# Linear attention: extra turns ahead of the first and last products, two block sums of the feed-forward weights made one column group earlier, and w_out split further ahead

## The chip, the cores and the metric

The kernel runs on one core of one Trainium2 chip. The metric is the time of one execution on the device in microseconds (us); lower is better. The times of a kernel are given as the median of its runs.

## The reference

One encoder layer on x of 512 x 2048 in float32. Cut to what matters:

```python
h = rmsnorm(x, attn_norm_w); proj = h @ w_in          # split: aq, ak, av, gq, gk, gv, gr, glr
attn_out = mixture_of_dilations(aq, ak, av)           # 16 heads of 64, three window patterns
log_a = log_sigmoid(glr @ gate_w + gate_b) / 16       # one for each direction, per key column
# gated linear attention, 4 heads, key width 128, value width 256, both directions summed:
#   S_t = diag(a_t) S_{t-1} + k_t^T v_t ;  o_t = q_t S_t
gla_out = rmsnorm_per_head(fwd + bwd) * gla_norm_w * silu(gr)
x = x + concat([attn_out, gla_out]) @ w_out           # w_out: 2048 x 2048
h = rmsnorm(x, ffn_norm_w)
x = x + (silu(h @ w_gate) * (h @ w_up)) @ w_down      # hidden width 5632
return rmsnorm(x, final_norm_w)
```

## The kernel before

**Products.** A float32 operand is split into two rounded halves, hi and lo, and a product is made as hi·hi + hi·lo + lo·hi: three matmuls, for the output jobs lines L346, L347 and L348. The hi half is a copy on ScalarE (ACT, L237), the lo half a subtraction on VectorE (DVE, L218). L347 is the matmul that reads the lo half of the weight. Gate and up, later, use products of blocks that are first added up; the sums of a weight piece are `Blocks.sums` (DVE, L1414 to L1416), its halves `Blocks.split` (ACT L1427, DVE L1432).

**Stages.** The attention's v projection to about 95 us; further projections of w_in to 345; attention and the linear attention's q, k and v projections to 612; the output projection to 843; gate and up to about 1715; down and the last norm to the end. The change lies in the output projection. It has column groups of 512 columns, each with 16 row blocks k. The first half of k (the attention's part) of groups 1, 2 and 3 comes first (612 to 715 us), then group 0 whole (to 770), then the second half of k (the linear attention's part) of groups 1, 2 and 3 (770 to 794, 794 to 817, 817 to 843). One step i of a job takes one k through four banks, so four units of three matmuls each. A job's banks are added to the residual by DVE (L1302, four of them, in `evac_out`).

**What runs beside it.** The four heads of linear attention are generators, `gla(h)`. `turns(…, APART)` interleaves them with a distance of 12 turns; after each bank of a job the rate (`RATES`) gives a quarter of so many turns, so a `yield` in `gla` is a place where other work is put in between, on every engine. A head does in this order: gate logits on TensorE (PE, L923); Abs, Exp, Ln on ACT (L933 to L935) with L936 on DVE; `less` (L945), `scan` (L951), `centre` (L963 to L966), exponents (ACT L973 to L975), `times` (L982) on DVE; for each direction the **first products** L1015 and transposes L1018 on PE, masked by L1021 on DVE and copied by ACT (L1025), added by L1029; `sums` (L1040 on PE), `decays` (L1049 on ACT), `chain` (L1059 on DVE); the **last products** L1087 on PE; squares and the norm (ACT L1095, DVE L377 to L386, ACT L1103); eight transposes L1110 on PE and the gate by L1113 on DVE; and the halves of the result (DVE L902), urgent. v comes back from DRAM by `load_gv` (POOL, L855).

Another side job makes block sums of later weights and stores them in DRAM (DVE L1483, POOL L1485).

**What sets the order.** Each engine runs its queue in the order in which the program issued it. Which bank of PSUM (`ps`) or buffer a step gets is decided when the program is built, by which one was put back first. `Job.lead(i)` says how many halves of the weight are split ahead of step i; `AHEAD` is 3. `before_out(c)` is called ahead of each step of the second halves and places gate's and up's loads (`ff.load`, SyncE L1395), sums and splits; a call of `ff.sums` on halves is six DVE instructions.

Of the kernel before, what the change touches and what calls it, by code (L numbers as in the profile page):

```python
# [26 lines left out]
KT = D // P  # L27
# [85 lines left out]
def put(*slots):  # L113
    for s in slots:
        if s.home is not None:
            s.home.free.append(s.i)


def layer(nc, tc, x, attn_norm_w, w_in, rel_table, gw_f, gb_f, gw_b, gb_b, gla_norm_w, w_out,
# [7 lines left out]
    with tc.manual_schedule(), \  # L127
# [43 lines left out]
        def tables(name):  # L171
            if state["set"] != name:
                state["set"] = name
                act.preload_act_table_set(name)
# [69 lines left out]
        AHEAD = 3  # L244

        def piece512(w, col, kt):

            ws = w if isinstance(w, list) else [(w, col)]
            n = 512 // len(ws)
            segs = []  # L250
            for i, (wi, c) in enumerate(ws):
                src = wi[kt * P:(kt + 2) * P, c:c + n].rearrange("(k p) c -> p k c", p=P)
                segs.append((src, lambda t, i=i, n=n: t.rearrange("p (k c) -> p k c", k=2)[:, :, i * n:(i + 1) * n]))
            return segs
# [9 lines left out]
        def run_urgent():  # L264
            while urgent:
                try:
                    next(urgent[0])
                    break
                except StopIteration:
                    urgent.popleft()  # L270
# [26 lines left out]
        def job(kind, pieces, kts, acts, evac, rate=0.0, before=None, start=None, limit=None):  # L297

            j = Job()
            j.kind, j.kts, j.acts, j.evac, j.rate, j.before, j.start, j.limit = \  # L300
                kind, kts, acts, evac, rate, before, start, limit
            j.first = len(st.halves)
            st.add(pieces)
            j.n = len(st.halves) - j.first
            jobs.append(j)
            return j
# [205 lines left out]
        def squares(c, t, tiles, ss, at_=None):  # L512
            junk = s2.get()
            m = c + (4 * t if at_ is None else at_)
            act.activation(junk.t, tiles[t].t, AF.Square, accum_out=ss[:, m:m + 1])
            put(junk)
# [314 lines left out]
        def evac_gqk(pr):  # L831
            def f(banks):
                for i in range(4):
                    t = s2.get()
                    if i < 2:
                        dve.scalar_tensor_tensor(t.t, banks[i].t, P ** -0.5, rb[1].t,
                                                 op0=OP.mult, op1=OP.mult)
                    else:
                        dve.tensor_tensor(t.t, banks[i].t, rb[1].t, op=OP.mult)
                    put(banks[i])  # L840
                    pool.dma_start(out=gqd[4 * pr + i], in_=t.t)
                    put(t)
            return f
# [69 lines left out]
        def gla(h):  # L913
# [15 lines left out]
            for d in range(2):  # L929
                tables(EXP_LN)  # L930
                bcol = wcol[:, (B_F, B_B)[d] + h:(B_F, B_B)[d] + h + 1]
                l, m = s2.get(), s2.get()
                act.activation(l.t, zs[d].t, AF.Abs, bias=bcol)  # L933
                act.activation(l.t, l.t, AF.Exp, scale=-1.0)
                act.activation(l.t, l.t, AF.Ln, bias=1.0)  # L935
                dve.tensor_scalar(m.t, zs[d].t, bcol, 0.0, op0=OP.add, op1=OP.min)  # L936
                put(zs[d])
                las.append((m, l))
                yield
            fs = [sc[d][:, 0:3] for d in range(2)]  # L940
            gs, qs, ks = [], [], []

# [68 lines left out]
            for d in range(2):  # L1011
                a, tr = ps.get(), ps.get()
                for b in range(4):
                    c = slice(b * P, (b + 1) * P)
                    mm(a.t[:, c], ks[d].t[:, c], qs[d].t[:, c], start=True, stop=True)  # L1015
                for b in range(4):
                    c = slice(b * P, (b + 1) * P)
# [37 lines left out]
            def chain(d):  # L1055
                for n, b in list(enumerate(orders[d]))[1:]:
                    at_ = b if d == 0 else b - 1
                    s = stts[d].t[:, n]
                    dve.scalar_tensor_tensor(s, stts[d].t[:, n - 1], fs[d][:, at_:at_ + 1], s,  # L1059
                                             op0=OP.mult, op1=OP.add)  # L1060
# [7 lines left out]
            decays(1)  # L1068
            yield
            chain(1)  # L1070
            yield

            on = s4.get(F32, [P, 4, 256])
# [3 lines left out]
            for i in range(2):  # L1077
                o = ps.get()
                for b in (2 * i, 2 * i + 1):
                    c = slice(b * P, (b + 1) * P)  # L1080
# [19 lines left out]
            for i in range(2):  # L1100
                for b in (2 * i, 2 * i + 1):
                    c = slice((b % 2) * 256, (b % 2 + 1) * 256)
# [120 lines left out]
                fr.late()  # L1223

        n_front = len(jobs)
        RATES = (2.5, 4.0)
        APART = 12
        for pr in range(2):
            seg = [(w_in, C_GQ + pr * 256), (w_in, C_GK + pr * 256)]
            job("A", [piece512(seg, None, k) for k in range(0, KT, 2)], list(range(KT)), acts_h,  # L1230
                evac_gqk(pr), rate=RATES[0], start=gstart if pr == 0 else None,
                before=None if pr else before_first, limit=3)
            job("B", [piece512(w_in, C_GV + pr * 512, k) for k in range(0, KT, 2)], list(range(KT)), acts_h,
                evac_gv(pr), rate=RATES[0],
                before=(lambda i: load_gates() if i == 12 else None) if pr else None)
# [63 lines left out]
        def evac_out(c, part=False):  # L1299
            def f(banks):  # L1300
                for t in range(4):
                    dve.tensor_tensor(x1[c][t].t, x1[c][t].t, banks[t].t, op=OP.add)  # L1302
                    put(banks[t])
                if not part:
                    urgent.append(rest())

            def rest():
                yield
                for t in range(4):
                    squares(c, t, x1[c], ss2)  # L1310
                    pool.dma_start(out=xd[4 * c + t], in_=x1[c][t].t)
                if c == 3:
                    dve.tensor_reduce(sum2, ss2.rearrange("p (t c) -> p t c", c=4), op=OP.add,
                                      axis=mybir.AxisListType.X)
                    rstd_of(sum2, 4, rstd2, 1.0 / D, scr)
                fs_ = {}
                for q in (2 * c, 2 * c + 1):
                    fs_[q] = s4.get(F32, [P, 2, 512])
                    for k in range(2):
                        weighted(x1[c], 2 * q + k, W_FFN, fs_[q].t[:, k])  # L1320
                    yield
                put(*x1.pop(c))
                if c == 3:
                    rb[2] = rows_of(rstd2)
                for q in (2 * c, 2 * c + 1):
                    yield from pair_operands(q, fs_.pop(q))
            return f

        def before_out(c):
            def f(i):  # L1330
                run_urgent()
                if c >= 2:
                    i += 8 * (c - 2)
                    if i >= 6:
                        ff.most = 3 if i < 9 else 5
                        ff.load()
                    if i in (8, 9, 11, 12, 14):
                        ff.sums(ff.n_sums, halves=True)
                    if i in (13, 15):
                        ff.split((i - 13) // 2)  # L1340
            return f

        def start_out(c):
            def f():
                if c == 1:
                    free_h()
                if c != 1:
                    load_res(c)
            return f
# [4 lines left out]
        def job_out(c, a, z, evac, **kw):  # L1354
            return job("B", [piece512(w_out, c * 512, k) for k in range(a, z, 2)], list(range(a, z)),
                       lambda k: mixh[k], evac, limit=3, **kw)

        for c in (1, 2, 3):
            job_out(c, 0, 8, evac_out(c, True), rate=RATES[1], start=start_out(c),
                    before=(lambda i: load_res(1) if i == 3 else None) if c == 1 else None)  # L1360
        n_in = len(jobs)
        jobs[n_front + 3].lead = lambda i: AHEAD + (i > 11) + (i > 13)
        j = job_out(0, 0, KT, evac_out(0), rate=RATES[1], start=start_out(0))
        for j in jobs[n_front:]:
            j.fine = True
        j.drop = lambda k: drop_mix(k) if k < 8 else None
        for j in jobs[n_front + 4:]:
            j.lead = lambda i: AHEAD + 2
        for c in (1, 2, 3):
            j = job_out(c, 8, KT, evac_out(c), rate=1.0, before=before_out(c))  # L1370
        j.drop = drop_mix
# [276 lines left out]
        ff = Feed()  # L1648
# [375 lines left out]
        for c in range(4):  # L2024
            j = job("B", [piece512(w_down, c * 512, k) for k in (0, 2)], list(range(4)),
                    lambda k: gT[k], evac_down(c), before=before_down(c))
# [6 lines left out]
        for c in range(4):  # L2033
            j = job("B", [piece512(w_down, c * 512, k) for k in (LAST - 4, LAST - 2)], list(range(LAST - 4, LAST)),
                    lambda k: gT[k], evac_later(c), before=before_later(c))
# [143 lines left out]
```

## Time and profile before

| what | value |
|---|---|
| median of 3 runs (lowest, highest) | 2171.98 us (2170.52, 2172.09) |
| profiled execution | 2170.55 us, span 2168.8 us |
| PE busy | 99% of the span, 12682 instructions |
| DVE, ACT, POOL busy | 84%, 56%, 16% |
| granted clock of PE, mean | 0.999 |

The profile is of one execution. Busy time is what an engine's instructions took; PE's matmuls are pipelined and their ends are modelled. A row of a wait has the waiting engine and line, what ended the wait, and then the time in all, the number of waits and the longest. A row of the timeline has the start, the duration, the engine, the line, output and input, the number of instructions that it joins, and in brackets the idle time of the engine before it and what ended that.

### The profile page before, as it was taken

What the parts mean: (1) busy time and instruction counts of PE and PEld (TensorE: products, weight loads), DVE (VectorE), ACT (ScalarE), POOL (GpSimd) and SP (SyncE); (2) the same over time, 40 slices, a digit from 0 to 9 for tenths busy, and PEclk for the clock granted to TensorE, in tenths of its full rate; (3) what the DMA queues carried; (4) which work ended last, traced back from release to release, by engine and by line L of the source; (5) the groups of instructions that cost most, each with busy time, mean ns of one, the idle gap of its engine ahead of it and who ended that gap; (6) DMA issues with size and microseconds to landing.
All of it is one profiled execution on the core that took longest, in us unless ns stands there. A gap on an engine that the chain in (4) does not pass through costs nothing.

```text
span 2168.8 us, 34922 instructions
## 1 busy us (share of the span) xinstructions
PE 2150.9 (99%) x12682; PEld 1897.8 (88%) x12682; DVE 1821.4 (84%) x3153; ACT 1221.1 (56%) x2228; POOL 355.6 (16%) x495
## 2 busy tenths in 40 slices
PE   9999999999999999999999999999999999999998
PEld 7888887888878888888888888888888899999987
DVE  6689996777768768899899999998989888898885
ACT  8455554677666446455555555555555655555562
POOL 0011213111011110011222112211221120021300
PEclk9999999999999999999999999999999999999999
DMA  6467779546475763477777677777776985576982
GB/s 202 140 176 182 175 186 251 151 134 179 136 260 180 258 224 119 141 178 180 188 177 186 182 182 191 173 184 178 179 199 176 267 207 174 179 182 155 284 309 78
DMA packets 264699, 405.71 MB, mean 187 GB/s; under 512 B 19341, under 2 KB 163389, under 8 KB 264526
## 3 DMA queue, kind: packets, MB, share of 16 engines
q1 hardware_dynamic: 206366, 274.59, 40.0%
q0 software_dynamic: 57840, 128.35, 26.7%
q8 instruction: 100, 1.64, 0.3%
q14 instruction: 73, 0.60, 0.1%
q10 hardware_dynamic: 320, 0.53, 0.1%
HBM read 287.47 MB, written 66.39 MB: 163 GB/s over the span
## 4 chain that ended last, share of the span: by engine, by line
PE 58%; DVE 0%; DMA 0%; issue 0%; ACT 0%; DVEq 0%; ACTq 0%
PE ps L1523 24%; PE ps L1509 12%; PE ps L1882 5%; PE ps L1881 5%; PE ps L1880 5%; PE ps L348 1%; PE ps L346 1%; PE ps L347 1%; PE ps L2076 1%; PE ps L2075 1%; PE ps L2077 1%; DMA gd<-b 0%; DVE b L1432 0%; DVE a L2108 0%; DVE a L1543 0%
## 5 line engine op out<-in xcount | busy, mean ns | idle before, releaser
L1427 ACT CAST b<-b 128x768 fp32r<-128x768 f32 (+1 forms) x569 | 518.9, 944 | 379.9 <-DVE b L1432 184.0
L1432 DVE TENSOR_TENSOR b<-b,b 128x768 fp32r<-128x768 f32 (+1 forms) x569 | 597.4, 1085 | 33.3 <-ACT b L1427 21.7
L1523 PE MATMUL ps<-b,b 128*128 128x512 f32 x1656 | 484.1, 393 | 0.4 <-ACT b L1427 0.2
L1523 PE MATMUL ps<-a,b 128*128 128x512 f32 x1368 | 401.0, 394 | 0.6 <-ACT b L1427 0.4
L1523 PEld LDWEIGHTS ps<-b,b 128*128 128x128 f32 x1656 | 280.8, 188 | 32.0 <-ACT b L1427 0.7
L1509 PEld LDWEIGHTS ps<-b,b 128*128 128x128 f32 x1656 | 271.4, 190 | 39.2
L1509 PE MATMUL ps<-b,b 128*128 128x256 f32 x1656 | 296.8, 280 | 0.0
L1509 PEld LDWEIGHTS ps<-a,b 128*128 128x128 f32 x1368 | 227.3, 189 | 37.0 <-DVE b L1432 0.8
L1523 PEld LDWEIGHTS ps<-a,b 128*128 128x128 f32 x1368 | 228.1, 189 | 23.1 <-ACT b L1427 0.6
L1509 PE MATMUL ps<-a,b 128*128 128x256 f32 x1368 | 245.6, 280 | 0.3 <-DVE b L1432 0.3
L1414 DVE TENSOR_TENSOR b<-b 128x512 f32<-128x512 f32 x260 | 178.2, 685 | 17.4 <-DMA b<-in_w_down_dram 6.4
L1880 PE MATMUL ps<-b,b 128*128 128x256 f32 x624 | 176.6, 283 | 0.0
L1881 PE MATMUL ps<-b,b 128*128 128x256 f32 x624 | 176.6, 283 | 0.0
L1882 PE MATMUL ps<-b,b 128*128 128x256 f32 x624 | 176.6, 283 | 0.0
L1880 PEld LDWEIGHTS ps<-b,b 128*128 128x128 f32 x624 | 119.8, 192 | 0.0
L1881 PEld LDWEIGHTS ps<-b,b 128*128 128x128 f32 x624 | 119.8, 192 | 0.0
L1882 PEld LDWEIGHTS ps<-b,b 128*128 128x128 f32 x624 | 119.8, 192 | 0.0
L346 PE MATMUL ps<-b,b 128*128 128x512 f32 x296 | 119.0, 402 | 0.3 <-ACT b L455 0.3
L1415 DVE TENSOR_TENSOR b<-b,b 128x256 f32<-128x256 f32 x260 | 110.5, 425 | 9.0
L1416 DVE TENSOR_TENSOR b<-b,b 128x256 f32<-128x256 f32 x260 | 110.6, 425 | 8.9
L348 PE MATMUL ps<-b,b 128*128 128x512 f32 x296 | 115.7, 391 | 0.2 <-DVE b L459 0.2
L347 PE MATMUL ps<-b,b 128*128 128x512 f32 x296 | 115.5, 390 | 0.0
(301 smaller groups left out, 4184.4 us busy)
## 6 DMA issues: line engine op xcount, KB each, us to landing
b<-in_w_gate_dram SPq DMA_DIRECT2D x109, 512.0 KB, 4.1
b<-in_w_up_dram SPq DMA_DIRECT2D x88, 512.0 KB, 4.3
b<-in_w_down_dram SPq DMA_DIRECT2D x88, 512.0 KB, 5.3
b<-a POOLq DMA_DIRECT2D x162, 256.0 KB, 4.5
b<-in_w_in_dram SPq DMA_DIRECT2D x78, 512.0 KB, 3.8
b<-in_w_out_dram SPq DMA_DIRECT2D x32, 512.0 KB, 5.2
gd<-b POOLq DMA_DIRECT2D x22, 512.0 KB, 4.0
b<-gd SPq DMA_DIRECT2D x22, 512.0 KB, 7.8
```

What stands on the lines that cost most here:

```text
L346: mm(o, xh.t[:, c], wh.t[:, w], start=first and not on, stop=False, skip_group_check=on)
L347: mm(o, xh.t[:, c], wl.t[:, w], start=False, stop=False, skip_group_check=on)
L348: mm(o, xl.t[:, c], wh.t[:, w], start=False, stop=last, skip_group_check=on)
L1414: dve.tensor_tensor(s_[:, :, 0:2], r[:, :, 1:3], r[:, :, 0:1].to_broadcast(shape), op=OP.add)
L1416: dve.tensor_tensor(s_[:, :, 3], s_[:, :, 2], r[:, :, 3], op=OP.add)
L1427: act.copy(o, src)
L1432: dve.tensor_tensor(o, src, h, op=OP.subtract)
L1509: mm(o, wl, xh, start=False, stop=end, skip_group_check=True)
L1523: mm(o.rearrange("p (s t) -> p s t", s=2), wh, x_, start=first and p == 0, stop=False, skip_group_check=True)
L1880: mm(o, xh[:, t], wh, start=first and h == 0, stop=False, skip_group_check=True)
L1881: mm(o, xh[:, t], wl, start=False, stop=False, skip_group_check=True)
L1882: mm(o, xl[:, t], wh, start=False, stop=last, skip_group_check=True)
```

## The change

A head gets one turn more ahead of its last products, and the first head two turns more behind its Ln and ahead of `less`. The rate of turns goes from 4.0 to 4.2. For the first halves of groups 1 to 3 and for group 0, w_out is split up to seven halves ahead, where it was five. Two calls of `ff.sums` that stood at steps 0 and 4 of group 3 stand at steps 0 and 2 of group 1; so that their pieces are there, two loads are issued at step 12 of group 0. Each engine has the same number of instructions of each kind as before; their order, and with it some buffers and banks, changes.

```diff
@@ gla @@
                 las.append((m, l))
                 yield
+            if h == 0:
+                yield
+                yield
             fs = [sc[d][:, 0:3] for d in range(2)]
...
             chain(1)
+            yield
             yield
 
             on = s4.get(F32, [P, 4, 256])
...
-        RATES = (2.5, 4.0)
+        RATES = (2.5, 4.2)
         APART = 12
...
         def before_out(c):
             def f(i):
                 run_urgent()
+                if c == 1 and i in (0, 2):
+                    ff.sums(ff.n_sums, halves=True)
                 if c >= 2:
                     i += 8 * (c - 2)
                     if i >= 6:
                         ff.most = 3 if i < 9 else 5
                         ff.load()
-                    if i in (8, 9, 11, 12, 14):
+                    if i in (9, 11, 14):
                         ff.sums(ff.n_sums, halves=True)
...
+        def load_first(i):
+            if i == 12:
+                ff.most = 2
+                ff.load()
+
...
-        j = job_out(0, 0, KT, evac_out(0), rate=RATES[1], start=start_out(0))
+        j = job_out(0, 0, KT, evac_out(0), rate=RATES[1], start=start_out(0), before=load_first)
...
         for j in jobs[n_front + 4:]:
-            j.lead = lambda i: AHEAD + 2
+            j.lead = lambda i: AHEAD + 4
         for c in (1, 2, 3):
             j = job_out(c, 8, KT, evac_out(c), rate=1.0, before=before_out(c))
```

## The prediction

> Line numbers here are those of the kernel before; "unit" means three matmuls L346, L347, L348 of an output job, counted from the start of the program, so unit 278 means "after 278 units". Times are from the start of the span.
>
> **What bounds the kernel now.** I read the page's engine shares first, then what the tensor engine waits for, then the same by stretches.
>
> ```profile
> PE 2150.9 (99%) x12682; PEld 1897.8 (88%) x12682; DVE 1821.4 (84%) x3153; ACT 1221.1 (56%) x2228; POOL 355.6 (16%) x495
> ```
> ```profile
> PE ps L1087 <- DVE b L1059: 2.1, 2, 1.8
> PE ps L347 <- DVE a L218: 1.7, 2, 1.0
> PE ps L1015 <- DVE a L982: 1.6, 1, 1.6
> ```
> ```profile
> 600.00:650.00 50.00, 46.57 (x221) 38.62 (x220) 33.17 (x62) 31.59 (x58) 9.60 (x18) 1.00 0.77 263
> ...
> 800.00:850.00 50.00, 48.31 (x248) 40.69 (x247) 45.35 (x108) 26.82 (x62) 5.42 (x10) 1.00 0.49 159
> ...
> 2150.00:2169.00 19.00, 10.34 (x57) 8.85 (x56) 12.36 (x30) 4.61 (x16) 0.00 (x0) 0.90 0.31 110
> ```
>
> PE is the bound: it is busy for 2150.9 of 2168.8 us (a stretch's row has its length, then the busy time of PE, PEld, DVE, ACT and POOL with their instructions, and PE's clock). Of the 17.9 us that remain 8.5 lie in the last stretch (which reaches 0.2 us past the end) that the change does not touch, 3.4 and 1.7 in the two where it does most. The change keeps the number of instructions of each kind on every engine, so it can only win or lose idle time of PE. The three waits shown are the ones that it is near: 2.1 + 1.7 + 1.6 = 5.4 us by name in five places. Each costs some 0.16 us more than its name says, as this row shows:
>
> ```profile
> 627.65 0.39 PE L347 MATMUL ps<-b,b 128*128 128x512 f32 x1
> 627.88 0.39 PE L348 MATMUL ps<-b,b 128*128 128x512 f32 x1
> 629.87 1.16 PE L1015 MATMUL ps<-a,a 128*128 128x128 f32 x8 [1.60 <-DVE a L982]
> ```
>
> One matmul follows the other after 0.23 us, so L1015 could have started at 628.11; it started at 629.87, 1.76 us late for a wait called 1.60. Five waits therefore cost 5.4 + 5 x 0.16 = 6.2 us, and that is the most that can be won. A change by 0.2% is 4.3 us, about the least that a measurement of this kernel can tell from none; below I count in these terms. A unit is 3 x 0.23, near 0.68 us.
>
> **The change part by part.** What decides is the order in which the changed program's instructions stand on PE and DVE, because a turn that is added moves PE's product and DVE's work for it alike.
>
> *First products of head 0 (L1015).* They move from unit 278 to 281: PE arrives 3 x 0.68 = 2.04 us later, at 630.15. But w_out is split two halves further ahead from here on, and so two more copies L237 stand ahead of the head's first activation on ACT, and on DVE three more L218 stand ahead of its first subtraction L945 (two of them beside the wait for ACT) and one more L1483.
>
> ```profile
> 629.00 1.12 ACT L237 CAST b<-b 128x512 fp32r<-128x512 f32 x2
> ```
> ```profile
> 619.88 0.75 DVE L936 TENSOR_SCALAR a<-ps,wcol 128x512 f32<-128x512 f32 x1 [1.08 <-ACT a L933]
> 620.54 0.41 DVE L1483 TENSOR_TENSOR b<-b 128x256 f32<-128x256 f32 x1
> 620.88 0.69 DVE L945 TENSOR_TENSOR a<-a,a 128x512 f32<-128x512 f32 x1
> ...
> 628.52 1.29 DVE L982 TENSOR_TENSOR a<-a,a 128x512 f32<-128x512 f32 x2
> ```
>
> Two L237 are 2 x 0.51 us (1.12 for two that overlap by 0.1), so L933 and all behind it come 1.02 us later. On DVE one L218 (0.60, as one of the two L982) and one L1483 (0.41) are not covered, another 1.0 us. L945 starts at 620.88 + 2.0 = 622.9. From there to the end of the second L982 DVE worked without a gap, 629.81 - 620.88 = 8.93 us; one L1483 less stands in between, so 8.5 us, and L982 ends near 631.5. PE waits 631.5 - 630.15 = 1.35 us and the same 0.05 of signalling as before: 1.4 in place of 1.76, a gain of 0.36. The two extra yields buy almost nothing, since the deeper lead and the turns spend on DVE what PE gives.
>
> Head 0's second L1015 (unit 283) now takes the PSUM bank that L1021's first instruction frees. That stands behind the third and fourth L982, two L1483 and an L218 (1.2 + 0.8 + 0.6 us behind 631.5, then 0.74 for itself, 634.8) where PE arrives near 634.2: **+0.6** (0 to 1).
>
> *Last products of head 0 (L1087).* They go from unit 293 to 297, their predecessors L1040 from 286 to 290, so the distance stays seven units. Ahead of the last L1059 DVE now has more.
>
> ```profile
> 641.58 2.47 DVE L1302 TENSOR_TENSOR b<-b,ps 128x512 f32<-128x512 f32 x4
> ...
> 644.57 1.00 DVE L1059 SCALAR_TENSOR_TENSOR b<-b,small 128x256 f32<-128x256 f32 x2
> 645.49 0.68 DVE L945 TENSOR_TENSOR a<-a,a 128x512 f32<-128x512 f32 x1
> 646.21 1.22 DVE L951 TENSOR_TENSOR_SCAN a<-a,a 128x512 f32<-128x512 f32 x1
> ...
> 648.65 0.15 DVE L963 TENSOR_TENSOR small<-a 128x3 f32<-128x3 f32 x1
> ...
> 649.52 0.68 DVE L945 TENSOR_TENSOR a<-a,a 128x512 f32<-128x512 f32 x1
> ```
> ```profile
> 639.93 1.46 PE L1040 MATMUL ps<-b,a 128*128 128x256 f32 x6
> 641.04 0.58 PE L346 MATMUL ps<-b,b 128*128 128x512 f32 x1
> ...
> 646.03 0.59 PE L1087 MATMUL ps<-b,a 128*128 128x256 f32 x2
> 648.45 1.78 PE L1087 MATMUL ps<-b,a 128*128 128x256 f32 x7 [1.83 <-DVE b L1059]
> ```
>
> Behind the last L1302, which waits for PE's unit 288 (done near 641.7 in the new order, since the second L1040, 1.1 us from 639.93 to the next unit, now comes after it), stand an L218, the second head's two L945 and two L951, its L963 to L966 (648.65 to 649.52), an L1483, the first L1059 pair, another L218 and the last pair: 0.6 + 0.7 + 1.15 + 0.9 + 0.6 + 0.4 + 1.0 + 1.15 + 0.6 + 1.0 = 8.1 us, from 642.5 to 650.6. PE had been ready at 646.46 (two matmuls of 0.22 behind 646.03) and is ready at 646.46 + 4 x 0.68 - 0.36 + 0.6 = 649.4. It waits 1.2 in place of 1.99: **-0.8**. If the L1302 end as before, at 644.05, the wait is 3.1 us; I take 1.2, since they wait for nothing but PE and DVE's own order.
>
> *A bank that two transposes share.* The moved steps change which PSUM bank each product is given. For heads 0 and 1 the two groups of four transposes L1110 now go to one bank, where they had two, so the second four wait until the first L1113 has read it.
>
> ```profile
> 661.99 1.04 PE L1110 MATMUL ps<-idn,b 128*128 128x128 f32 x8
> ```
> ```profile
> 662.63 1.41 DVE L1113 SCALAR_TENSOR_TENSOR a<-ps,wcol,a 128x512 f32<-128x512 f32 x2 [3.31 <-PE ps L1110]
> ```
>
> Before, L1113 began 0.64 us after the first transpose and one took 0.75; the second four can start 1.45 us after the first, where they started after 0.44 (issued 0.11 apart). That is **+1.0** for each of two heads, if DVE stands waiting as it did then (3.31 us idle); more if it is late, nothing less. For head 0 the next L1040 (unit 311, one unit behind) takes the bank that the second L1113 frees: 1.4 us after the fifth transpose, PE is there after 1.1: **+0.3** (0 to 0.7). Head 1's has three units between and waits for nothing. Its own last products (now eight units behind L1040, were six) waited for nothing and have 1.2 us to spare.
>
> *Last products of head 2*
>
> ```profile
> L902 DVE TENSOR_TENSOR b<-a,b 128x512 fp32r<-128x512 f32 x4 | 2.7, 685 | 0.0
> ```
>
> They waited the other 0.3 (0.46 with the refill). They go from six to eight units behind L1040 (1.36 us for PE), but two L902 (0.69 each) and an L951 (1.22) now stand ahead of the last L1059 and one L218 (0.6) behind it: -1.36 + 2.5 - 0.6 = +0.5; the bank wait just before holds PE 1.0 and DVE only 0.6. **+0.1** (-0.4 to +1).
>
> *First products of head 3.* The second four go to unit 353 and take the bank of the first four, which L1021 frees.
>
> ```profile
> 716.67 0.69 DVE L218 TENSOR_TENSOR b<-b,b 128x512 fp32r<-128x512 f32 x1
> 717.61 0.74 DVE L1021 COPY_PREDICATED a<-masks,ps 128x512 f32<-128x512 uint32 x1 [0.26 <-POOL a L1010]
> ```
>
> In the new order L1021 is behind the four L1302, the last of which waits for unit 352, and an L218: 0.2 + 0.6 + 0.6 + 0.7 = 2.1 us after unit 352. PE is there after one unit, 0.68: **+1.4** (0.7 to 2).
>
> *Column groups 1 to 3, second halves.* Two of the five calls that make gate's and up's block sums leave the third group for group 1.
>
> ```profile
> 834.00 0.42 DVE L1414 TENSOR_TENSOR a<-b 128x256 f32<-128x256 f32 x1
> ...
> 835.98 0.68 DVE L218 TENSOR_TENSOR a<-b,a 128x512 fp32r<-128x512 f32 x1
> ```
> ```profile
> 836.72 0.50 PE L347 MATMUL ps<-a,b 128*128 128x512 f32 x1 [0.69 <-DVE a L218]
> ```
>
> A call is six instructions, 835.98 - 834.00 = 1.98 us. DVE runs 4 us earlier where PE waits for L218, whose two waits cost 1.7 + 0.32 = **-2.0**. Both vanish unless ACT's copies come late. In group 1 the 4 us meet this:
>
> ```profile
> 768.66 2.73 DVE L1302 TENSOR_TENSOR b<-b,ps 128x512 f32<-128x512 f32 x4 [8.89 <-PE ps L348]
> ...
> 774.64 0.42 DVE L479 TENSOR_TENSOR b<-b 128x256 f32<-128x256 f32 x1 [1.06 <-ACT b L404]
> ```
>
> The first call is behind the L1302, for which DVE stood idle until 768.66, so it can't use that idle time. It uses the 1.4 us around L479, and the rest, 2.6 us, is lateness of the L218 that follow; the tightest is ready near 786 where PE needs it at 788.5. Nothing is lost there, with 2.5 us to spare. The extra loads of w_gate are issued before 756, the sums come after 771.
>
> *POOL's queue.* The two loads of v (L855) now stand behind L1485, which waits for an L1483 near 628.9.
>
> ```profile
> 616.86 1.08 POOL L855 DMA_DIRECT2D b<-gvd  x2
> 628.90 0.54 POOL L1485 DMA_DIRECT2D sd<-b  x1 [10.96 <-DVE b L1483]
> ```
> ```profile
> DMA to landing us min/median/max: 3.9/6.5/9.8
> ```
>
> Issued at 629.4 and 630.0, they land by 639.8 at the latest; L1040 wants the first at 639.5 and the second 0.9 later. Nothing by the rows; what a later landing costs is one of the rivals.
>
> The sum: -0.36 + 0.6 - 0.8 + 2.0 + 0.3 + 0.1 + 1.4 - 2.0 = +1.2 us. The profiled run took 2170.55 us, its span 2168.8 and 1.75 around it; the median of the three runs is 2171.98, 1.4 above. So 2171.8 for a profiled run and 2173.2 us for the median.
>
> **The rivals.**
> *Faster.* The turns clear the waits, as DVE gets ahead by more than I count, and the banks' waits lie beside them. At most 6.2 us: 2165.8. For it speaks that every named wait has a step in the change; against it that seven units stay seven and that the shared banks are in the order, not in the times. It needs 4.3 of the 6.2. 0.07.
>
> *Slower, by one mechanism: the sums of group 1 wait for their weights.* DVE takes its queue in order; if a w_gate piece is issued no earlier than in the run before (775.53) and lands after the median 4.1 us, the first sum that should run near 772 runs at 779.6, 7.6 us late. With 2.6 for the sums themselves, less the 2.5 spare, PE loses 7.7 us: 2180.9. It makes the kernel slower by 0.2% from 3.1 us on, that is from a landing after 775.
>
> ```profile
> 775.53 0.37 SPq L1395 DMA_DIRECT2D b<-in_w_gate_dram  x1
> ```
>
> Against it: the new order puts the issue before the loads of w_out that were issued at 757. 0.05. The Trainium skill (TensorE: Matmul & The Clock Gate, "What's actually happening") adds that PE's clock falls to half after some 3.4 us without work and comes back after as long a stretch of work, by an estimate from that page 1.7 us more in this rival and nothing in the forecast. By that the trace agrees as far as it goes: the clock is 1.00 in the stretches with waits of up to 1.8 us, and 0.90 only in the last.
>
> *Slower by a late load of v.* Its two transfers, issued at 629.4 and 630.0, fall into DVE's unbroken work, and get going only when DVE first idles, which before was for 0.99 us until 637.25:
>
> ```profile
> 637.25 0.75 DVE L936 TENSOR_SCALAR a<-ps,wcol 128x512 f32<-128x512 f32 x1 [0.99 <-ACT a L933]
> ```
>
> From 636.3 the median of 6.5 us ends at 642.8, 3.3 us after L1040 wants them: 2176.5. The Trainium skill (SBUF — State Buffer, "SBUF: two separate sides") states such a rule: descriptors of a transfer from GpSimd's queue can't be written while VectorE holds the port pair that both use, in a mode that takes both ports. No row here shows such a hold: with DVE busy for most of this time, no load of v landed later than 9.8 us after its issue. 0.03.
>
> *Slower by piling up.* The L1302 end at 644.05 (+1.9), head 2 is at its upper end (+0.9), the bank waits meet a late DVE (+1): 2177.0. 0.07.
>
> *It doesn't do what it says.* ACT's copies hold L347's waits in group 3 as they are: +2.0, 2175.2, still no change. 0.2, within "same".
>
> **How the numbers follow.** My forecast, no change that can be told (2168 to 2176.2), has 0.78 with the last rival in it; slower 0.15, faster 0.07. The range reaches from most of the terms at their low ends (all bounds taken together, 2169) to the pile-up (2177.5).
>
> **What would show it.** Right: the wait of L1015 for L982 near 1.2, of L1087 for L1059 below 1.5, new waits of L1110 for L1113 near 1 us twice, one of L1015 for L1021 over 1 us near 717, no wait of L347 for L218. Wrong: L1110 without a wait; a wait in 770 to 795; a sum of named waits under 3 us or over 10 in 600 to 850.

## The result: 4.5 us slower, inside the range, with one cause that the forecast did not have

The changed kernel takes 2175.07 us (median of 22 runs, 2173.1 to 2178.01), the kernel before 2170.55 us (22 runs, 2169.22 to 2172.86). The ratio is 1.0019, 95% interval 1.0013 to 1.0026. The forecast was 2173.2 us in a range of 2168 to 2176.2, called no change that can be told. The time lies in the range, near its upper end: 4.5 us of loss, where 1.2 were worked out. The call itself does not quite hold, since the whole interval lies above 1: with 22 runs of each, a loss of 0.13% to 0.26% can be told.

In the changed kernel most line numbers are higher: L1015 is now L1018, L1018 is L1021, L1021 is L1024, L982 is L985, L1040 is L1043, L1059 is L1062, L1087 is L1091, L1103 is L1107, L1110 is L1114, L1113 is L1117, L1302 is L1306, L1414 is L1425. What PE waits for in the changed kernel, with the total, the number and the longest:

```profile
PE ps L1018 <- DVE a L985: 1.9, 1, 1.9
PE ps L1091 <- DVE b L1062: 1.9, 2, 1.2
PE ps L1114 <- DVE a L1117: 1.7, 2, 0.8
PE ps L1018 <- DVE small L383: 1.4, 1, 1.4
PE ps L346 <- DVE b L472: 1.4, 1, 1.4
...
PE ps L923 <- ACT b L1107: 0.6, 2, 0.4
...
PE ps L1018 <- DVE a L1024: 0.3, 1, 0.3
```

Five of these rows are new, and the row of L347 for L218 is gone. The one of L346 for L472 is at 7 us, in a part that the change does not touch, and a second profile of the same kernel does not have it: in the first one, behind this wait, PE's clock was halved for 3.41 us. Its first 600 us are 2.4 us longer than in the second, and that is in its span of 2175.0 (2176.77 us with what lies around). By stretches (length, then the busy time of PE, PEld, DVE, ACT, POOL, and the clock), two of the kernel before and then those of the changed kernel:

```profile
650.00:700.00 50.00, 50.00 (x256) 42.54 (x255) 42.91 (x87) 32.52 (x80) 9.45 (x18) 1.00 0.55 186
700.00:750.00 50.00, 49.70 (x242) 41.90 (x241) 36.36 (x80) 26.35 (x67) 5.87 (x11) 1.00 0.68 227
```
```profile
600.00:650.00 50.00, 47.81 (x231) 39.75 (x229) 34.40 (x63) 34.75 (x63) 10.63 (x20) 1.00 0.76 260
650.00:700.00 50.00, 46.95 (x234) 38.65 (x232) 37.69 (x79) 29.35 (x74) 7.97 (x15) 1.00 0.55 181
700.00:750.00 50.00, 47.28 (x227) 39.63 (x228) 37.57 (x80) 24.32 (x65) 5.94 (x11) 1.00 0.55 181
...
800.00:850.00 50.00, 50.00 (x239) 41.58 (x238) 39.80 (x88) 29.03 (x63) 5.91 (x11) 1.00 0.52 177
```

The stretch from 800 lost nothing any more (1.7 us before). PE now idles 3.0 and 2.7 us in the two stretches from 650 to 750, where it had idled 0.0 and 0.3.

In the table each place counts what PE lost there: the start of the late matmul, less the start of the one before, less their usual distance. The second profile of the changed kernel is in brackets where it differs.

| place (lines of the kernel before) | before | changed | forecast |
|---|---|---|---|
| head 0, first products L1015 | 1.76 | 2.09 (1.92) | 1.4 |
| head 0, second L1015, bank | 0 | 0.43 | 0.6 |
| head 0, last products L1087 | 1.99 | 1.34 | 1.2 |
| head 0, transposes L1110, shared bank | 0 | 1.01 | 1.0 |
| L1040 behind them, bank | 0 | 0.32 | 0.3 |
| head 3, gate logits L923, two banks | 0 | 1.06 | none |
| head 1, transposes L1110, shared bank | 0 | 1.01 | 1.0 |
| head 2, last products L1087 | 0.47 | 0.89 | 0.6 |
| head 3, second L1015, bank | 0 | 1.58 | 1.4 |
| group 3, L347 for L218 | 2.01 | 0 | 0 |
| sum | 6.23 | 9.73 (9.56) | 7.5 |

So 3.3 to 3.5 us of the loss are seen in place. The whole stage, from the 3201st of PE's matmuls, ahead of it, to the 4501st, behind it, takes 262.7 us before and 266.6 (266.4) us in the changed kernel: 3.8 to 3.9 us are lost in it, some 0.4 of them in no place of the table.

### The profile page after: what moved, and what is told of

It is laid out like the page before. It is cut to its first block, busy times and chain, and to the rows that moved or that the text cites. A ratio compares the mean times of both kernels' runs of the same rounds, so it can differ in the third digit from the quotient of the medians.

```text
span 2175.0 us, 34925 instructions
## 1 busy us (share of the span) xinstructions
PE 2154.0 (99%) x12682; PEld 1899.1 (87%) x12682; DVE 1820.7 (84%) x3153; ACT 1222.1 (56%) x2228; POOL 354.9 (16%) x495
## 4 chain that ended last, share of the span: by engine, by line
PE 58%; DVE 0%; DMA 0%; issue 0%; ACT 0%; DVEq 0%; ACTq 0%
PE ps L1534 24%; PE ps L1520 12%; PE ps L1893 5%; PE ps L1892 5%; PE ps L1891 5%; PE ps L347 1%; PE ps L346 1%; PE ps L348 1%; PE ps L2088 1%; PE ps L2087 1%; PE ps L2086 1%; DMA gd<-b 0%; DVE b L1443 0%; DVE a L2119 0%; DVE a L1554 0%
## 5 line engine op out<-in xcount | busy, mean ns | idle before, releaser
L1534 PE MATMUL ps<-b,b 128*128 128x512 f32 x1656 | 484.1, 393 | 0.4 <-ACT b L1438 0.2
L1425 DVE TENSOR_TENSOR b<-b 128x512 f32<-128x512 f32 x260 | 178.2, 686 | 17.5 <-DMA b<-in_w_down_dram 7.0
L346 PE MATMUL ps<-b,b 128*128 128x512 f32 x304 | 122.5, 403 | 1.4 <-DVE b L472 1.4
L348 PE MATMUL ps<-b,b 128*128 128x512 f32 x304 | 119.3, 392 | 0.2 <-DVE b L459 0.2
L347 PE MATMUL ps<-b,b 128*128 128x512 f32 x304 | 119.2, 392 | 0.2 <-DVE b L473 0.2
```

What stands on the lines that cost most here:

```text
L346: mm(o, xh.t[:, c], wh.t[:, w], start=first and not on, stop=False, skip_group_check=on)
L347: mm(o, xh.t[:, c], wl.t[:, w], start=False, stop=False, skip_group_check=on)
L348: mm(o, xl.t[:, c], wh.t[:, w], start=False, stop=last, skip_group_check=on)
L1425: dve.tensor_tensor(s_[:, :, 0:2], r[:, :, 1:3], r[:, :, 0:1].to_broadcast(shape), op=OP.add)
L1534: mm(o.rearrange("p (s t) -> p s t", s=2), wh, x_, start=first and p == 0, stop=False, skip_group_check=True)
```

## The experiments

The theory: the moved steps make two heads in flight hold the four PSUM banks that the output job leaves free, so that PE waits for banks; the moved block sums pay 2 us back. The rival: the deeper split of w_out fills the queues of ACT and DVE ahead of the heads' chains, so that the extra turns buy nothing. Each kernel was timed beside the kernel before: 2170.88 us for the first four, 2171.05 for the next four, 2171.30 for the last three.

**The block sums alone.**

```diff
 kernel before
+                if c == 1 and i in (0, 2):
+                    ff.sums(ff.n_sums, halves=True)
-                    if i in (8, 9, 11, 12, 14):
+                    if i in (9, 11, 14):
+        (load_first, at step 12 of group 0)
```

> The kernel before with one part of the change alone: the two calls of the block sums stand in group 1 and their loads at step 12 of group 0. If the sums are a gain by themselves (my theory), the two waits of L347 for L218 in group 3 (0.85 and 1.16 us with the refill) vanish, no wait appears between 770 and 795 us, the waits of heads 0 and 2 stay as before, and the time is 2170.55 - 2.0 = 2168.5 us. The rival: they only move the wait to group 1, where L218 is late behind 4 us of sums; then PE waits between 780 and 795 and the time is 2170.5 or more.

2168.74 us, ratio 0.9990 (0.9981 to 0.9999). What PE waits for:

```profile
PE ps L1087 <- DVE b L1059: 2.1, 2, 1.8
PE ps L1015 <- DVE a L982: 1.6, 1, 1.6
```
```profile
770.00:795.00 25.00, 25.00 (x120) 20.96 (x119) 24.49 (x58) 13.48 (x30) 3.81 (x8) 1.00 0.54 184
```

The waits of the heads are as before and L347's for L218 is gone. DVE is busy for 24.5 of 25 us in group 1, yet PE is without a gap there. This part is a gain of 2.1 us, as forecast.

**The deeper split taken back.**

```diff
 changed kernel
-            j.lead = lambda i: AHEAD + 4
+            j.lead = lambda i: AHEAD + 2
```

> The changed kernel with w_out split two halves further ahead as before, not four; PE's order and its banks stay those of the changed kernel. If the deeper split is what keeps the turns from working (theory of the queues), the wait of head 0's first products for the last products of its inputs falls from 2.09 us to about 0.5 (two copies of 0.51 on ACT and one L218 of 0.6 gone ahead of it), head 0's last products wait 0.7 rather than 1.34, and the time is near 2173.0 us. If the shared banks are the cost (theory of the banks), their 5.4 us stay as they are whatever happens to these two: not below 2172.5 us, and 2175 if the two do not move either.

2173.74 us, ratio 1.0015 (1.0006 to 1.0024).

```profile
PE ps L1091 <- DVE b L1062: 1.9, 2, 1.2
PE ps L1114 <- DVE a L1117: 1.7, 2, 0.8
PE ps L1018 <- DVE small L383: 1.4, 1, 1.4
...
PE ps L1018 <- DVE a L985: 0.7, 1, 0.7
```

The first products lose 0.85 us in place of 2.09, so the deeper split costs 1.2 us there. The last products did not move (1.36 us; 0.7 was expected), and every bank's wait stayed the same to 0.01 us. The two times alone could not tell this, since their intervals overlap; the places do. Both theories hold a part; that of the banks has the larger.

**One turn less ahead of the last products.**

```diff
 changed kernel
             chain(1)
-            yield
             yield
```

> The changed kernel without the extra turn ahead of the last products. In the order built so, the eight last transposes of heads 0 and 1 have two banks again, while head 0's last products are five units behind their predecessors rather than seven, and head 2's six rather than eight. Theory of the banks: the two waits of 1.01 us of the transposes for the product by the gate vanish, and the waits of the last products for the chain grow by up to 1.4 us each; 2174 to 2175 us in all. Theory of the queues: nothing is won by the banks and the last products lose 1.4 us twice: 2178 us.

2175.49 us, ratio 1.0022 (1.0013 to 1.0032).

```profile
PE ps L1090 <- DVE b L1062: 4.9, 3, 2.3
PE ps L1018 <- DVE a L985: 1.6, 1, 1.6
```
```profile
649.00:651.00 2.00, 0.40 (x2) 0.00 (x0) 2.00 (x3) 0.00 (x0) 0.00 (x0) 1.00 0.83 307
651.00:653.00 2.00, 1.28 (x3) 1.10 (x4) 1.86 (x7) 0.42 (x1) 0.00 (x0) 0.60 0.02 7
653.00:655.00 2.00, 2.00 (x6) 1.57 (x6) 2.00 (x4) 1.33 (x4) 0.00 (x0) 0.54 0.00 0
```

The transposes have two banks and lose 0.2 us in all, where it was 2.0. But the last products (L1090 here) lose 2.48, 1.56 and 1.36 us in heads 0, 1 and 2, and behind the longest of these the clock, the column after POOL's, is halved. That last step, 1.6 us, was in neither expectation, and the time is a little above the 2174 to 2175 of the theory of the banks. What the banks gave back the missing turn took, so the time stays. The turn was worth its place; what it did to the banks was not.

**The heads 13 turns apart.**

```diff
 changed kernel
-        APART = 12
+        APART = 13
```

> The changed kernel with one number changed: the heads start 13 turns apart, not 12. In the order built so, both groups of last transposes, and both groups of first products, have different banks in every head, and the gate logits of the next heads no longer stand just ahead of them. Theory of the banks: the waits for banks (1.01 twice, 0.32, 0.43, 1.58 and 0.56 + 0.50 us of the gate logits, 5.4 in all) are gone or nearly so, the waits of head 0 for its own chain (2.09 and 1.34) stay, and the time is 2169.7 to 2171 us, about that of the kernel before. Theory of the queues: the same instructions stand ahead on ACT and DVE, so the time stays at 2175 us.

2167.95 us, ratio 0.9987 (0.9978 to 0.9996).

```profile
PE ps L1018 <- DVE a L985: 1.6, 1, 1.6
...
PE ps L1114 <- ACT b L1107: 0.7, 1, 0.7
...
PE ps L1091 <- DVE b L1062: 0.3, 1, 0.3
```

All waits for banks are gone. One of 1.1 us in two steps appears, of head 1's transposes for their input from ACT, and the last products of head 0 lose 0.46 in place of 1.34. The same turns, split and sums are 7 us faster at this distance, more than the 4 to 5.4 us expected: head 0's and head 2's last products lose 0.9 us less each, which the banks alone did not promise. So one number moved more than the banks; that the 5.4 us of bank waits are gone is what the places show. The theory of the queues, which had 2175 here, is out as the main cause.

**The deeper split alone.**

```diff
 kernel before
-            j.lead = lambda i: AHEAD + 2
+            j.lead = lambda i: AHEAD + 4
```

> The kernel before with the deeper split of w_out alone. PE's order and banks are those of the kernel before. Theory of the queues: two copies more on ACT and two L218 more on DVE stand ahead of head 0's chain, as in the changed kernel, where taking them away cut the wait from 2.09 to 0.85 us; so the wait of the first products grows from 1.76 to about 3.0 us, the wait of the last products stays at 2.0, and the time is 2170.9 + 1.2 = 2172.1 us. The rival: the halves are split in time that ACT and DVE had to spare, the waits stay, 2170.9 us.

2175.26 us, ratio 1.0018 (1.0009 to 1.0027). Both expectations missed. The first products lose 3.33 us rather than 3.0, and then this follows:

```profile
628.00:631.00 3.00, 0.00 (x0) 0.00 (x0) 2.93 (x9) 2.00 (x5) 0.95 (x2) 1.00 1.06 376
631.00:633.00 2.00, 1.98 (x12) 1.99 (x13) 2.00 (x4) 0.27 (x1) 1.61 (x4) 0.67 1.08 370
633.00:635.00 2.00, 2.00 (x7) 1.61 (x6) 2.00 (x5) 1.10 (x2) 0.00 (x0) 0.50 1.07 379
```

The clock is 0.50: matmuls of the output job start 0.43 us apart until 635, where 0.23 is usual, some 1.7 us in all for a stretch of 3.41 us. ACT's part shows why the wait was longer than two copies make it:

```profile
619.79 0.62 ACT L237 CAST b<-b 128x512 fp32r<-128x512 f32 x1 [0.42 <-DMA gvd<-b]
```

The halves that are now split earlier are put where v's transfer to DRAM has not yet been read out, and the copy waits 0.42 us for it, with the head's second activation behind it. The longer wait (1.6 us more than before) and the halved clock make 3.2 of the 4.2 us between the medians; the rest was not found.

**Both: 13 turns and the split taken back.**

```diff
 changed kernel
-        APART = 12
+        APART = 13
-            j.lead = lambda i: AHEAD + 4
+            j.lead = lambda i: AHEAD + 2
```

> The changed kernel with the heads 13 turns apart and w_out split as far ahead as before. If the two costs are separate, the first products of head 0 wait 1.79 - 1.24 = 0.55 us, the other waits stay as with 13 turns alone (0.46 for the chain, 1.1 for head 2's transposes), and the time is 2167.95 - 1.2 = 2166.7 us. If the deeper split was of use elsewhere (group 3's L218 in time, say), a wait of L347 for L218 comes back and the time is 2168 us or more.

2166.83 us, ratio 0.9983 (0.9974 to 0.9991): the time is as expected of two separate costs. The first products lose 0.87 us, where 0.55 was expected, and the rest is as with 13 turns alone (the transposes that the expectation gives to head 2 are those of head 1). This is faster than both kernels.

**14 turns and three ahead of the first subtraction.**

```diff
 the last kernel
-        APART = 13
+        APART = 14
             if h == 0:
                 yield
                 yield
+                yield
```

> As the last, but with three more turns rather than two ahead of head 0's first subtraction and the heads 14 turns apart, which is the distance at which the order built has two banks for every pair of products again. PE reaches head 0's first products two units (1.4 us) later than with two turns, so that their wait goes, and the last products are seven units behind their predecessors as before. Theory of the banks: 2166 us, all waits of the heads together under 1.5 us. If a turn spends on DVE what PE gives, the wait stays near 0.5 us and the time near 2167 us.

2168.27 us, ratio 0.9989 (0.9980 to 0.9997), missed. The first products wait for nothing any more (0.18 us), but PE waits elsewhere (L1092 and L1307 are the lines L1091 and L1306 of the changed kernel):

```profile
PE ps L1092 <- DVE b L1307: 2.0, 1, 2.0
```
```profile
676.00:678.00 2.00, 1.59 (x5) 1.36 (x6) 2.00 (x4) 0.00 (x0) 0.00 (x0) 0.73 0.07 26
678.00:680.00 2.00, 2.00 (x7) 1.56 (x6) 1.97 (x6) 0.00 (x0) 0.00 (x0) 0.50 0.00 0
```

Head 1's last products now fall on the end of group 2's first half, where all four of the job's banks wait to be added, and lose 2.19 us and then the clock.

**13 turns without the turns.**

```diff
 the kernel with the block sums alone
-        APART = 12
+        APART = 13
```

> The kernel before with the block sums moved and the heads 13 turns apart; no extra turns, rate 4.0, w_out split as before. If the turns ahead of first and last products are a gain once the banks are clear, this keeps the waits of head 0 (1.76 and 2.0 us) and stays at 2168.5 us, that of the moved sums alone, 2 us above the kernel with turns. If the distance alone is the gain, it comes to 2166.7 us as well.

2169.74 us, ratio 0.9992 (0.9983 to 1.0001). The distance alone is not the gain.

```profile
PE ps L1087 <- DVE b L1302: 2.4, 1, 2.4
PE ps L1015 <- DVE a L982: 1.6, 1, 1.6
...
PE ps L1087 <- DVE b L1059: 0.3, 1, 0.3
```

The first products lose 1.77 us without the turns ahead of them, 0.87 with them: they are a gain once nothing else is in the way. The last products of head 0 have their wait cut without a turn (0.44 us; 2.0 was expected to stay), and head 1's fall on the group's end as in the kernel with 14: they lose 2.57 us, and the clock is halved behind them. Against the moved sums at 12 turns, 2168.74 us, the distance of 13 gains nothing here.

**The changed kernel again.**

> The changed kernel once more, for its second profile and for more times. In its first profile PE's clock was halved for 3.41 us at 8.5 us, where the kernel before has no such stretch, and the wait of 2.09 us for head 0's first products left the clock at 1.00; in three other kernels a wait of 2.2 to 3.3 us was followed by a halved stretch. If the waits alone make the change slower, the excess between 612 and 852 us is near 11.8 us again and the start without the halved stretch brings the profiled run near 2174.5 us. If a wait of 2.1 us is long enough for the clock in some runs, the excess is 1.7 us more in such a profile, and the times fall into groups some 1.7 us apart.

2174.89 us, ratio 1.0015 (1.0006 to 1.0024). The profiled run took 2174.89 us; its excess is the same place by place, and the clock is 1.00 behind the wait of 1.92 us:

```profile
630.00:632.00 2.00, 0.24 (x2) 0.05 (x1) 2.00 (x5) 1.27 (x4) 2.00 (x5) 1.00 1.08 364
632.00:634.00 2.00, 2.00 (x15) 1.91 (x16) 2.00 (x5) 1.36 (x3) 1.14 (x3) 1.00 1.06 398
```

The times show no clear groups. So the waits make the loss; whether the clock adds to some runs is open.

**13 turns, one half further ahead than the base distance.**

```diff
 the kernel with 13 turns and the split taken back
-            j.lead = lambda i: AHEAD + 2
+            j.lead = lambda i: AHEAD + 1
```

> Heads 13 turns apart, turns and sums of the change, and w_out split one half further ahead than the base distance, one less than in the kernel before (two before, four in the change). Theory of the queues: another copy of 0.51 us and an L218 fewer ahead of head 0's chain, so the 0.87 us that its first products still wait fall to about 0.3, 2166.3 us. If the halves then come too late for PE, waits of L347 for L218 or of L346 for the copy appear between 612 and 770 us, and the time is above 2167 us.

2167.03 us, ratio 0.9979 (0.9969 to 0.9989). The first products wait for nothing; instead this row comes, of 0.65 us at 787 us in group 1:

```profile
PE ps L347 <- DVE a L218: 0.5, 1, 0.5
```

The two cancel: no difference from the kernel with `AHEAD + 2` (2166.83 us) can be told.

**No turns at all.**

```diff
 changed kernel
-            if h == 0:
-                yield
-                yield
...
             chain(1)
-            yield
             yield
```

> The changed kernel without any of the extra turns: rate 4.2, deeper split and moved sums stay. The order built so has different banks for every pair of last transposes, and head 0's first products come after 277 units, four earlier than with the turns. Theory of the banks and queues together: no wait of the transposes for the product by the gate, but PE is at the first products 2.7 us earlier and waits some 4 us for them, which is long enough for the halved clock (1.7 us); with the 2.0 of the sums won, 2173 to 2175 us. If the turns are the only cause of the loss, the time is that of the moved sums, 2168.7 us.

2174.77 us, ratio 1.0013 (1.0004 to 1.0022), as the first expectation had it. No wait of the transposes is left. The first products lose 3.07 us (some 4 were expected), head 0's last products 2.52, and the clock is halved behind both:

```profile
PE ps L1087 <- DVE b L1059: 3.3, 3, 2.4
PE ps L1015 <- DVE a L982: 2.9, 1, 2.9
...
PE ps L1040 <- DVE b L1302: 0.9, 1, 0.9
```
```profile
631.00:633.00 2.00, 2.00 (x9) 1.68 (x8) 2.00 (x5) 1.10 (x2) 2.00 (x5) 0.56 1.06 369
...
653.00:655.00 2.00, 2.00 (x6) 1.61 (x5) 1.86 (x5) 1.11 (x5) 0.00 (x0) 0.50 0.40 153
```

So the change without its turns and the change with them cost the same, for different reasons: without them PE waits above all for the chains of head 0, with them above all for banks. One wait for a bank comes without them too, of 1.04 us, of L1040 behind the additions of group 3's banks. The rate of 4.2, which this kernel keeps, was not tried by itself.

## Why the prediction came out as it did

**The shared bank: right, to 0.01 us.** Head 0's rows of the timeline carry it, of PE and of DVE, in the changed kernel:

```profile
671.06 0.60 PE L1114 MATMUL ps<-idn,b 128*128 128x128 f32 x4
672.50 0.66 PE L1114 MATMUL ps<-idn,b 128*128 128x128 f32 x4 [0.84 <-DVE a L1117]
```
```profile
671.70 0.75 DVE L1117 SCALAR_TENSOR_TENSOR a<-ps,wcol,a 128x512 f32<-128x512 f32 x1 [2.52 <-PE ps L1114]
673.20 0.75 DVE L1117 SCALAR_TENSOR_TENSOR a<-ps,wcol,a 128x512 f32<-128x512 f32 x1 [0.75 <-PE ps L1114]
```

The second four start 1.44 us after the first; 1.45 was forecast. DVE idles 0.75 us in between: the two engines take turns on one bank. The cause is shown by the kernel with 13 turns, where the pairs have two banks and these waits are gone.

**Head 3's second first products: right** (1.58, forecast 1.4). DVE's rows are the forecast's chain: the additions of group 3's banks, an L218, and then the instruction that frees the bank. The wait's name, L383, is that of the instruction behind it.

```profile
722.89 1.38 DVE L1306 TENSOR_TENSOR b<-b,ps 128x512 f32<-128x512 f32 x2 [1.34 <-PE ps L348]
724.18 0.68 DVE L218 TENSOR_TENSOR b<-b,b 128x512 fp32r<-128x512 f32 x1
724.79 0.72 DVE L1024 COPY_PREDICATED a<-masks,ps 128x512 f32<-128x512 uint32 x1
```
```profile
725.65 1.13 PE L1018 MATMUL ps<-a,a 128*128 128x128 f32 x8 [1.41 <-DVE small L383]
```

**Head 0's last products, its two other waits for banks and the block sums: right** (1.34 for 1.2; 0.43 for 0.6 at the second first products and 0.32 for 0.3 at L1040; -2.01 for -2.0). The loads of v and of w_gate cost nothing, as argued; the rivals that hung on them did not occur.

**Head 3's gate logits: missed, 1.06 us, the largest error.** They moved three units forward, to ten units behind head 1's last products, and take the two banks that those had filled. ACT reads these twice, the second time in L1107, which has to wait for DVE's part of the norm and had not finished:

```profile
693.07 1.57 ACT L1107 ACTIVATE b<-ps,small 128x256 f32<-128x256 f32 x4 [2.32 <-DVE small L386]
```
```profile
693.96 0.50 PE L923 MATMUL ps<-a,a 96*128 96x512 f32 x1 [0.39 <-ACT b L1107]
694.69 0.50 PE L923 MATMUL ps<-a,a 96*128 96x512 f32 x1 [0.23 <-ACT b L1107]
```

The part "a bank that two transposes share" followed the banks of the products that the change names and not those of L923, which no line of the diff touches. It is the same mechanism at one place more; at 13 turns, where L923 is fifteen units behind again, the wait is gone.

**Head 0's first products: mis-sized, 2.0 for 1.4.** The step counted two copies on ACT but not that the second has to wait for a buffer (the row of 0.42 us above; 0.50 and 0.32 us in the two profiles of the changed kernel). In the second profile `less` starts 2.3 us later than before, where 2.0 was worked out, and from there DVE takes 8.7 us to the end of the second L985 rather than 8.5. The sign was wrong with it: a loss of 0.2 to 0.3, not a gain of 0.36; and the wait "near 1.2" that the prediction named as a sign of being right is 1.9 and 1.8. That the deeper split eats what the turns give is shown by its removal, 1.2 us.

**Head 2's last products: 0.89 for 0.6.** The step set 0.6 us of delay for DVE against 1.0 for PE at the bank just before; DVE's idle time there, at head 1's shared bank, is 0.75 as in head 0's rows above, and the remaining 0.15 was not traced.

With these three terms, 0.6 + 1.06 + 0.3, and the small ones the sum is 3.3 to 3.5 us in place of 1.2. The medians differ by 4.5 us in the first comparison and 3.6 in the second; up to 1 us is not found in any place, and stays open. The rival of a pile-up, 2177.0, had the right direction with the wrong places: the banks did not meet a late DVE, there was one clash more. The rival at 2175.2 hit the time by chance: the waits of L347 that it kept are gone.

**What was luck.** All three terms erred to the same side, and the range was wide enough to take it. The forecast of 2173.2 also stands on a median of three runs, 2171.98; the 22 runs give 2170.55, with which the same sum comes to 2171.8, 3.3 us below what was measured instead of 1.9. Three figures of the prediction do not follow from its own: the wait that it puts at 3.1 us for an end of the L1302 at 644.05 is 644.05 + 8.1 - 649.4 = 2.8; the pile-up is 2177.0 in one place and 2177.5 in another, both above the range that is said to reach to it; and the low bounds that it states add up to about 2171, not 2169.

## What to carry to other kernels

A turn put in between two steps of interleaved work moves not only its own wait but also who holds which bank at that time: list the banks that each step takes and frees in the new order, of all heads and not only of the lines in the diff, before counting what the turn gains. The distance between the interleaved heads is the knob that clears such clashes: 12 to 13 turns was worth 7 us with the turns in place, more than any part of the change, and nothing without them, where it brought a new clash. Take a change of several parts apart: here the moved sums alone win 2.1 us, the deeper split loses, and the turns win only at another distance.

## What the runs showed of the hardware

I had not expected PE's clock to fall at such short waits. In the output projection it was halved for 3.41 us behind losses of 2.19, 2.48, 2.52, 2.57, 3.07 and 3.33 us in one stretch, and was not behind 1.76, 1.92, 1.99 and 2.09; each time this cost 1.6 to 1.7 us (at the last products, eight matmuls some 0.21 us late apiece). It was also halved at the start of the changed kernel's first profile, behind a wait of 1.36 us and two of 0.16 shortly after it, so the length of one wait alone does not decide it. The Trainium skill (TensorE: Matmul & The Clock Gate, "What's actually happening") gives an idle window of about 3.4 us for it; the stretch of 3.41 agrees with the window, but a wait of two thirds of it was enough here. In these runs a wait of 2.19 us or more between matmuls was thus dear: the shortest cost nearly twice what it lasted.
